# Retention, heads 1 and 2: V and gate as seven half-size products, three quarters of whose weight sums are added by DMA

## The chip, the cores and the metric

The kernel runs on one core of one Trainium2 chip. A core has TensorE (matmul), VectorE, ScalarE, GpSimd (Pool) and SyncE (which here issues the loads), an on-chip memory (SBUF) of 128 partitions, a small accumulator memory (PSUM) that TensorE writes, and 16 DMA engines. The metric is device time of the one core, in microseconds, the median of several runs.

## The reference

A decoder trunk in float32: SEQ = 512 tokens, D_MODEL = 1024, one retention layer with an FFN, then one attention layer with an FFN. The change touches only the retention layer's projections. Each of four heads has 256 columns for q and k and 512 for v and for the gate g:

```python
def retention_mixer(h, w_in, w_out, gn_gain, pos):
    proj = h @ w_in
    q = proj[..., :dqk].reshape(B, S, RET_HEADS, RET_QK_DIM)
    k = proj[..., dqk:2 * dqk].reshape(B, S, RET_HEADS, RET_QK_DIM) * (RET_QK_DIM ** -0.5)
    v = proj[..., 2 * dqk:2 * dqk + dv].reshape(B, S, RET_HEADS, RET_V_DIM)
    g = proj[..., 2 * dqk + dv:]
    ...
    y = retention_chunkwise(q, k, v, log_gamma).astype(jnp.float32)
    mu = jnp.mean(y, axis=-1, keepdims=True)
    var = jnp.mean(jnp.square(y - mu), axis=-1, keepdims=True)
    yn = ((y - mu) * lax.rsqrt(var + GN_EPS)).reshape(B, S, dv) * gn_gain
    return (jax.nn.silu(g) * yn.astype(g.dtype)) @ w_out
```

For one head, v and g together are a 512 x 1024 matrix h times a 1024 x 1024 matrix [Wv Wg].

## The kernel before, in words

**Numbers.** A float32 operand is held as two parts, high and low, both of type float32r. One product is three matmuls: high by high, high by low, low by high (`mm3`). The normalised input stands transposed in `hT_hi` and `hT_lo` (8 depth tiles x 512 tokens).

**Weight units.** Weights come in units of 128 x 1024 (512 KB). `fetch` has SyncE load a unit into one of three `raw` buffers. `parts` has ScalarE cast it into `whi` and VectorE subtract to get `wlo`; there are five buffers of each (`WB`). So a load waits for the subtraction three units back, and a cast waits for the last matmul that reads the unit five back.

**Order.** The program's order on each engine is set by a list scheduler from the order in which the code emits work; each engine then executes its own list strictly in order and waits on semaphores. Generators interleave two streams of TensorE work: `_weave` lets `attend` of one head and the projections of the next alternate.

**Retention.** `project(h)` makes the gate (`proj_rows` with silu), q and k (`rotated`: two products of 128 columns, then a rotation on VectorE) and v (`proj_rows` with `split`). `proj_rows` takes four units of 256 depth rows and, for each, four blocks of 128 tokens; each block gathers in its own accumulator (`pm`, four buffers). `attend(h)` makes scores, decay, the product with v, the group norm (`r_gn` on Pool) and the gated result, transposed into `uh` and `ul`. `project_out(h)` multiplies these by four units of `w_out` and adds into `m`. The loop runs, for h = 1 to 3: `attend(h-1)` woven with the gate part of `project(h)`, the rest of `project(h)`, then `project_out(h-1)` (for the last two heads it comes later, woven with `attend(3)`). x stays in four tiles x0 to x3 from the start until the residual is added at the end of retention.

The loop that the change rewrites is this:

```python
for h in range(1, RET_HEADS):
    nxt, u = [], []
    fill = project(h, nxt)
    _weave(attend(h - 1, u, *cur), fill, 2.5)
    _run(fill)
    if h < last:
        _run(project_out(h - 1, u))
    cur = nxt
```

Of the kernel before, what the change touches and what calls it, by code (L numbers as in the profile page):

```python
# [10 lines left out]
F32 = mybir.dt.float32  # L11
# [64 lines left out]
def _run(gen):  # L76
    for _ in gen:
        pass
# [7 lines left out]
def _weave(gen, fill, per):  # L86

    due = 0.0
    for _ in gen:
        due += per  # L90
        while due >= 1:
            due -= 1
            next(fill, None)
# [3 lines left out]
def trunk(ctx: ExitStack, tc: tile.TileContext, a, out):  # L97
# [100 lines left out]
    def split(src, hi, lo, scale=None):  # L198
        if scale is None:
            nc.scalar.copy(out=hi, in_=src)  # L200
            nc.vector.tensor_sub(out=lo, in0=src, in1=hi.bitcast(F32))  # L201
        else:
            nc.scalar.activation(hi, src, AF.Copy, scale=scale)
            nc.vector.scalar_tensor_tensor(
                out=lo, in0=src, scalar=scale, in1=hi.bitcast(F32), op0=ALU.mult, op1=ALU.subtract
            )
# [212 lines left out]
    def retention(pool, post, then, ahead):  # L419
        w_in, w_out = a["ret_w_in"][0], a["ret_w_out"][0]  # L420
        with pool as tmp:
# [40 lines left out]
            def rotated(n0, name):  # L462
                t = tmp.tile([P, 2, SEQ], F32, name=name, tag=name, bufs=1)
                p = []
                for i in range(2):
                    pm = ps.tile([P, 512], F32, name="pm", tag="mm", bufs=4)
                    w = cols_unit(w_in, n0 + i * P)
                    for k in range(KT):
                        mm3(pm, [t[:, blk(k)] for t in w], (hi[:, k, :], lo[:, k, :]), k == 0, k == KT - 1)
                        yield  # L470
                    p.append(pm)
                u = [tmp.tile([P, SEQ], F32, name="t", tag="t", bufs=3) for _ in range(2)]
                for i in range(2):
                    nc.vector.tensor_mul(out=t[:, i, :], in0=p[i], in1=rot[:, 0, :])
                    nc.vector.tensor_mul(out=u[1 - i], in0=p[i], in1=rot[:, 1, :])
                nc.vector.tensor_sub(out=t[:, 0, :], in0=t[:, 0, :], in1=u[0])
                nc.vector.tensor_add(out=t[:, 1, :], in0=t[:, 1, :], in1=u[1])
                return t

            def project(h, res):  # L480
                g = [tmp.tile([P, 512], F32, name="g", tag="g", bufs=4) for _ in range(NB)]
                v = [[tmp.tile([P, 512], F32R, name=n, tag=n, bufs=4) for n in ("vh", "vl")] for _ in range(NB)]
                yield from proj_rows(
                    4 * D + h * 512, lambda b, p: nc.scalar.activation(g[b], p, AF.Silu), first=h == 0
                )
                if h == 0:
                    nc.sync.dma_start(out=rot, in_=a["rot"])
                    load_cols(0)
                    load_cols(1)
                q = yield from rotated(h * 256, "q")  # L490
                k = yield from rotated(D + h * 256, "k")
                yield from proj_rows(2 * D + h * 512, lambda b, p: split(p, *v[b]))
                res += [q, k, v, g]

            def attend(h, u_, q, k, v, g):
                tag = "po" if h < last else "mm"
# [77 lines left out]
            _run(project(0, cur))  # L574
            for h in range(1, RET_HEADS):
                nxt, u = [], []
                fill = project(h, nxt)
                _weave(attend(h - 1, u, *cur), fill, 2.5)
                _run(fill)
                if h < last:  # L580
                    _run(project_out(h - 1, u))
                cur = nxt
            fill = project_out(last - 1, u)
            u = []
# [559 lines left out]
```

## Time and profile before

| | us |
|---|---|
| median of 3 runs | 1696.15 (1696.0 to 1696.19) |
| the profiled execution, its own time | 1696.22 |
| its span, first to last instruction | 1694.4 |
| TensorE busy, by the page | 1675.3 |
| VectorE busy | 1088.6 |
| head 1's attend to head 2's begin (181.57 to 282.17) | 100.60 |

The page gives busy time by engine, the span in 40 slices, the chain of work that ended last, and the costliest groups of instructions. Matmuls are pipelined, so their recorded durations overlap and their pitch is read from the starts. In a group's row the output stands left of the arrow. Retention takes the span up to about 434 us; its four attends begin at 80.98, 181.57, 282.17 and 360.80 us.

### The profile page before, as it was taken

Reading aid. Unit: us, or ns where it says so; the run is one execution under the profiler, and the core shown is the slowest. Engines: PE = TensorE matmul, PEld = TensorE weight load, DVE = VectorE, ACT = ScalarE, POOL = GpSimd, SP = SyncE. Lnnn points to the kernel's source line nnn. Section 1 sums busy time; section 2 is a strip of 40 time slices with the busy share of each in tenths; the row PEclk is TensorE's granted clock in tenths of the full one; section 3 lists DMA queues with packets and bytes.
Section 4 is the critical chain, followed back from the end, with each engine's and each line's share of the span. In section 5 each row is a group of like instructions: output and inputs, shape, how many; then the busy total and the mean of one; then the engine's idle time right before and its main releaser. Section 6 shows DMA issues by size and latency. Waiting matters only on the chain.

```text
span 1694.4 us, 21845 instructions
## 1 busy us (share of the span) xinstructions
PE 1675.3 (99%) x8494; PEld 1388.9 (82%) x8494; DVE 1088.6 (64%) x1758; ACT 662.8 (39%) x1170; POOL 335.8 (20%) x241
## 2 busy tenths in 40 slices
PE   8999999999999999999999999999999999999998
PEld 6888888887888888888888888888887888888886
DVE  4554545557675777968856466556565865777785
ACT  5332322325445343334254244244254545443441
POOL 1000000001100000024456666565530300000000
PEclk9999999999999999999999999999999999999999
DMA  6422223214514323332322222222221633243141
GB/s 208 126 81 88 81 95 91 82 63 137 175 62 125 112 72 114 99 119 80 111 75 75 76 75 78 77 71 81 80 75 49 196 105 112 63 124 114 36 149 50
DMA packets 208567, 164.52 MB, mean 97 GB/s; under 512 B 5246, under 2 KB 182350, under 8 KB 208463
## 3 DMA queue, kind: packets, MB, share of 16 engines
q1 hardware_dynamic: 208462, 163.12, 31.0%
q8 instruction: 67, 1.10, 0.3%
q14 instruction: 38, 0.30, 0.1%
HBM read 156.81 MB, written 6.29 MB: 96 GB/s over the span
## 4 chain that ended last, share of the span: by engine, by line
PE 93%; DVE 3%; issue 2%; POOL 1%; ACT 1%; DMA 0%; SPq 0%; POOLq 0%; DVEq 0%; ACTq 0%
PE pm L210 22%; PE pm L212 22%; PE pm L211 22%; PE po L210 6%; PE po L211 6%; PE po L212 6%; PE sc L881 2%; PE po L991 2%; PE pt L971 2%; PE s L504 1%; DVE wlo L171 1%; POOL r_rms L217 1%; DVE x L354 1%; ACT junk L223 1%; PE y L210 1%
## 5 line engine op out<-in xcount | busy, mean ns | idle before, releaser
L210 PE MATMUL pm<-hT_hi,whi 128*128 128x512 f32 (+1 forms) x1424 | 544.6, 382 | 0.0
L211 PE MATMUL pm<-hT_lo,whi 128*128 128x512 f32 (+1 forms) x1424 | 537.9, 378 | 1.8 <-DVE hT_lo L201 1.8
L212 PE MATMUL pm<-hT_hi,wlo 128*128 128x512 f32 (+1 forms) x1424 | 538.1, 378 | 1.5 <-DVE wlo L171 1.5
L171 DVE TENSOR_TENSOR wlo<-raw,whi 128x1024 fp32r<-128x1024 f32 x299 | 398.5, 1335 | 212.9 <-ACT whi L170 211.2
L170 ACT CAST whi<-raw 128x1024 fp32r<-128x1024 f32 x299 | 313.1, 1051 | 496.7 <-PE pm L211 254.5
L212 PEld LDWEIGHTS pm<-hT_hi,wlo 128*128 128x128 f32 x1424 | 267.9, 188 | 52.0 <-DVE wlo L171 1.9
L210 PEld LDWEIGHTS pm<-hT_hi,whi 128*128 128x128 f32 x1424 | 268.1, 188 | 50.5 <-issue 2.7
L211 PEld LDWEIGHTS pm<-hT_lo,whi 128*128 128x128 f32 x1424 | 268.2, 188 | 50.2 <-DVE hT_lo L201 3.0
L160 POOL TENSOR_TENSOR raw<-raw,cols 128x1024 f32<-128x1024 f32 x72 | 144.3, 2007 | 465.7 <-DVE al L201 302.1
L210 PE MATMUL pm<-whi,hT_hi 128*128 128x512 f32 (+1 forms) x384 | 141.9, 369 | 0.0
L211 PE MATMUL pm<-wlo,hT_hi 128*128 128x512 f32 (+1 forms) x384 | 136.6, 356 | 0.0
L212 PE MATMUL pm<-whi,hT_lo 128*128 128x512 f32 (+1 forms) x384 | 136.6, 356 | 0.0
L227 POOL TENSOR_SCALAR v_rms<-ss 128x1 f32<-128x1 f32 x31 | 19.9, 643 | 466.1 <-ACT junk L223 450.4
L273 DVE TENSOR_TENSOR m<-po,m 128x512 f32<-128x512 f32 x112 | 75.2, 687 | 40.4 <-PE po L212 39.7
L210 PE MATMUL po<-whi,ah 128*128 128x512 f32 x224 | 87.3, 390 | 0.0
L212 PE MATMUL po<-whi,al 128*128 128x512 f32 x224 | 87.2, 389 | 0.0
L211 PE MATMUL po<-wlo,ah 128*128 128x512 f32 x224 | 87.1, 389 | 0.0
L210 PEld LDWEIGHTS pm<-whi,hT_hi 128*128 128x128 f32 x384 | 72.9, 190 | 11.6 <-issue 1.0
L211 PEld LDWEIGHTS pm<-wlo,hT_hi 128*128 128x128 f32 x384 | 72.9, 190 | 10.9 <-DVE wlo L171 0.7
L212 PEld LDWEIGHTS pm<-whi,hT_lo 128*128 128x128 f32 x384 | 72.8, 190 | 10.7 <-DVE hT_lo L201 0.3
L217 POOL TENSOR_TENSOR r_gn<-v_gn,nhalf 128x1 f32<-128x1 f32 x16 | 8.8, 548 | 357.4 <-DVE v_gn L534 357.4
L612 DVE SCALAR_TENSOR_TENSOR conv<-pm,cols,conv 128x511 f32<-128x511 f32 x88 | 65.7, 746 | 7.9 <-ACT conv L609 6.7
(163 smaller groups left out, 2182.5 us busy)
## 6 DMA issues: line engine op xcount, KB each, us to landing
raw<-in_ffn_w_up SPq DMA_DIRECT2D x88, 512.0 KB, 3.8
raw<-in_att_w_kv SPq DMA_DIRECT2D x48, 512.0 KB, 3.9
raw<-in_ret_w_in SPq DMA_DIRECT2D x47, 512.0 KB, 3.8
raw<-in_ffn_w_down SPq DMA_DIRECT2D x44, 512.0 KB, 3.4
raw<-in_att_w_q SPq DMA_DIRECT2D x24, 512.0 KB, 3.8
raw<-in_ret_w_out SPq DMA_DIRECT2D x16, 512.0 KB, 3.3
away<-x SPq DMA_DIRECT2D x8, 512.0 KB, 3.8
x<-away SPq DMA_DIRECT2D x8, 512.0 KB, 4.6
```

Source lines behind the costliest of these rows:

```text
L160: nc.gpsimd.tensor_mul(out=dst, in0=dst, in1=gain.unsqueeze(2).broadcast_to(list(src.shape)))
L170: nc.scalar.copy(out=hi, in_=raw)
L171: nc.vector.tensor_sub(out=lo, in0=raw, in1=hi.bitcast(F32))
L210: nc.tensor.matmul(o, lhsT=l[0], rhs=r[0], start=start, stop=False)
L211: nc.tensor.matmul(o, lhsT=l[0], rhs=r[1], start=False, stop=False)
L212: nc.tensor.matmul(o, lhsT=l[1], rhs=r[0], start=False, stop=stop)
L217: behind.append(nc.gpsimd.tensor_tensor(out=r, in0=v, in1=nhalf, op=ALU.pow).ins)
L273: nc.vector.tensor_add(out=dst, in0=src, in1=dst)
L612: nc.vector.scalar_tensor_tensor(out=t[:, d:], in0=pg[:, : SEQ - d], scalar=cw(i, f), in1=t[:, d:], op0=ALU.mult, op1=ALU.add)
L881: nc.tensor.matmul(pm[h][:, i, c], lhsT=q, rhs=k, start=True, stop=True)
L971: nc.tensor.transpose(out=pt[:, h, n, :], in_=p[:, h, :], identity=ident)
L991: nc.tensor.matmul(dst, lhsT=v, rhs=p, start=i == 0 and g == 0, stop=i == 7)
```

## The change

Heads 1 and 2 compute v and gate as a 2 x 2 block product. The rows are halved (tokens 0 to 255 and 256 to 511), the depth is halved, and the columns are halved into v and gate. Seven products of half size, numbered 1 to 7, replace eight. Products 1, 2 and 4 take blocks of h as they are. Products 3, 5, 6 and 7 take sums and differences of blocks of h (`block_sums`). These are made once, while head 0 projects, and kept split in the tiles of x, of the gains and of `h`; x is loaded again while head 3 projects, and the two gains too are loaded later.

On the weights' side the signs are chosen so that only plain sums occur: W11 + W12 (product 5), that plus W22 (6), that plus W21 (4), and W12 + W22 (7). The first is added by VectorE into the tile `t1`. W12 is copied into `t3` by ScalarE. The other three sums come from DMAs issued by Pool that add onto `t1` and `t3` as they land (`onto`), in halves of 512 KB, six in each head. Each sum is split again by `parts`. `evac` puts the products together: v and gate gather in float32 tiles, the gate's with its sign turned, which the silu undoes by scale -1.

The turn of a head changes as well: `attend(h-1)` is now woven with q and k of head h (`keys_queries`), then comes product 1, then `project_out(h-1)`, then products 3, 2, 5, 7, 6 and 4. Head 3 still uses `project`, and head 0 too.

```diff
@@ -488,9 +488,138 @@
                     load_cols(0)
                     load_cols(1)
                 q = yield from rotated(h * 256, "q")
+                if h == 0:
+                    block_sums(0)
                 k = yield from rotated(D + h * 256, "k")
+                if h == 0:
+                    block_sums(1)
                 yield from proj_rows(2 * D + h * 512, lambda b, p: split(p, *v[b]))
                 res += [q, k, v, g]
+            sums = []
+            def block_sums(c):
+                if c == 0:
+                    for i in range(4):
+                        sh = const.tile([P, 4, 256], F32R, name=f"s{i}", tag=f"x{i}")
+                        if i < 2:
+                            sl = norm.tile([P, 4, 256], F32R, name="sl", tag="gain", bufs=2)
+                            sums.append((sh, [sl[:, 0:2, :], sl[:, 2:4, :]]))
+                        else:
+                            sl = [norm.tile([P, 2, 256], F32R, name="sl", tag="h", bufs=HB) for _ in range(2)]
+                            sums.append((sh, sl))
+                e, o = slice(c * 2, c * 2 + 2), slice(4 + c * 2, 6 + c * 2)
+                t0, t1 = slice(0, SEQ // 2), slice(SEQ // 2, SEQ)
+                n = [tmp.tile([P, 512], F32, name="t", tag="t", bufs=3).rearrange("p (k n) -> p k n", k=2) for _ in range(3)]
+                whole = lambda dst, k, ts: nc.vector.tensor_add(
+                    out=dst, in0=hi[:, k, ts].bitcast(F32), in1=lo[:, k, ts].bitcast(F32)
+                )
+                put = lambda i, src: split(src, sums[i][0][:, e, :], sums[i][1][c])
+                whole(n[0], e, t1)
+                whole(n[1], o, t1)
+                nc.vector.tensor_sub(out=n[1], in0=n[1], in1=n[0])
+                put(0, n[1])
+                whole(n[2], e, t0)
+                nc.vector.tensor_sub(out=n[0], in0=n[2], in1=n[0])
+                put(2, n[0])
+                nc.vector.tensor_add(out=n[1], in0=n[1], in1=n[2])
+                put(1, n[1])
+                whole(n[2], o, t0)
+                nc.vector.tensor_sub(out=n[2], in0=n[1], in1=n[2])
+                put(3, n[2])
+            def v_gate(h, res):
+                cols_ = 2 * D + h * 512, 4 * D + h * 512
+                g = [tmp.tile([P, 512], F32, name="g", tag="g", bufs=4) for _ in range(NB)]
+                v = [[tmp.tile([P, 512], F32R, name=n, tag=n, bufs=4) for n in ("vh", "vl")] for _ in range(NB)]
+                res += [v, g]
+                load = lambda j, c, u: fetch(cols_of(w_in, cols_[c], 4, (j * 4 + u * 2) * P))
+                kept = {}
+                def onto(t, j, c, u):
+                    nc.gpsimd.dma_start(
+                        out=t[:, u, :].rearrange("p (k n) -> p k n", k=2),
+                        in_=cols_of(w_in, cols_[c], 4, (j * 4 + u * 2) * P),
+                        accum_op=ALU.add,
+                    )
+                def left(i, k, r):
+                    if i in (1, 2, 4):
+                        ts = slice((i == 4) * 256 + r * P, (i == 4) * 256 + (r + 1) * P)
+                        return [t[:, k + 4 * (i != 1), ts] for t in (hi, lo)]
+                    sh, sl = sums[{5: 0, 6: 1, 7: 2, 3: 3}[i]]
+                    return sh[:, k, blk(r)], sl[k // 2][:, k % 2, blk(r)]
+                def evac(i, r, pm):
+                    if i in (1, 3, 5):
+                        if i == 1:
+                            kept[i, r] = tmp.tile([P, 512], F32, name="t", tag="t", bufs=3)
+                        else:
+                            kept[i, r] = g[r + (2 if i == 5 else 0)]
+                        nc.scalar.copy(out=kept[i, r], in_=pm)
+                    elif i in (2, 4):
+                        t = tmp.tile([P, 512], F32, name=f"c{r}", tag=f"s{'hl'[r]}0", bufs=1)
+                        nc.vector.tensor_add(out=t, in0=pm, in1=kept[1, r])
+                        split(t, *v[r + (2 if i == 4 else 0)])
+                    elif i == 7:
+                        kept[7, r] = tmp.tile([P, 512], F32, name=f"c{r}", tag=f"s{'hl'[r]}0", bufs=1)
+                        nc.scalar.copy(out=kept[7, r], in_=pm)
+                    else:
+                        s1, s3, s5, s7 = (kept[j, r] for j in (1, 3, 5, 7))
+                        nc.vector.tensor_sub(out=s1, in0=s1, in1=pm)
+                        nc.vector.tensor_add(out=s5, in0=s5, in1=s1)
+                        nc.vector.tensor_add(out=s3, in0=s3, in1=s5)
+                        nc.scalar.activation(s3, s3, AF.Silu, scale=-1.0)
+                        nc.vector.tensor_add(out=s5, in0=s5, in1=s7)
+                        nc.vector.tensor_add(out=s1, in0=s1, in1=s7)
+                        nc.scalar.activation(s5, s5, AF.Silu, scale=-1.0)
+                def product(i, w):
+                    for r in range(2):
+                        pm = ps.tile([P, 512], F32, name="pm", tag="mm", bufs=4)
+                        for k in range(4):
+                            mm3(pm, left(i, k, r), [t[:, half(k % 2)] for t in w[k // 2]], k == 0, k == 3)
+                        evac(i, r, pm)
+                product(1, [parts(load(0, 0, u)) for u in range(2)])
+                yield
+                w3 = [parts(load(1, 1, u)) for u in range(2)]
+                w2 = [parts(load(1, 0, u)) for u in range(2)]
+                t1, t3 = (
+                    tmp.tile([P, 2, D], F32, name=n, tag=tag, bufs=1) for n, tag in (("t1", "uh"), ("t3", "ul"))
+                )
+                for u in range(2):
+                    r11, r12 = load(0, 0, u), load(0, 1, u)
+                    nc.scalar.copy(out=t3[:, u, :], in_=r12)
+                    nc.vector.tensor_add(out=t1[:, u, :], in0=r11, in1=r12)
+                    onto(t3, 1, 1, u)
+                product(3, w3)
+                w5 = [parts(t1[:, u, :]) for u in range(2)]
+                product(2, w2)
+                for u in range(2):
+                    onto(t1, 1, 1, u)
+                w7 = [parts(t3[:, u, :]) for u in range(2)]
+                product(5, w5)
+                w6 = [parts(t1[:, u, :]) for u in range(2)]
+                for u in range(2):
+                    onto(t1, 1, 0, u)
+                product(7, w7)
+                product(6, w6)
+                w4 = [parts(t1[:, u, :]) for u in range(2)]
+                product(4, w4)
+                yield
+            def keys_queries(h, res):
+                q = yield from rotated(h * 256, "q")
+                k = yield from rotated(D + h * 256, "k")
+                res += [q, k]
 
             def attend(h, u_, q, k, v, g):
                 tag = "po" if h < last else "mm"
@@ -574,11 +703,21 @@
             _run(project(0, cur))
             for h in range(1, RET_HEADS):
                 nxt, u = [], []
-                fill = project(h, nxt)
-                _weave(attend(h - 1, u, *cur), fill, 2.5)
-                _run(fill)
                 if h < last:
+                    fill = keys_queries(h, nxt)
+                    _weave(attend(h - 1, u, *cur), fill, 2.5)
+                    _run(fill)
+                    vg = v_gate(h, nxt)
+                    next(vg)
                     _run(project_out(h - 1, u))
+                    _run(vg)
+                else:
+                    fill = project(h, nxt)
+                    _weave(attend(h - 1, u, *cur), fill, 2.5)
+                    _run(fill)
+                    for b in range(NB):
+                        x[b] = const.tile([P, D], F32, name=f"x{b}", tag=f"x{b}")
+                        nc.sync.dma_start(out=x[b], in_=a["x"][blk(b), :])
                 cur = nxt
             fill = project_out(last - 1, u)
             u = []
```

Two engines show how the listed order moves. First Pool, from the last two group norms of head 0's attend to head 1's; `r_gn` is the group norm's reciprocal root, and the brackets say which engine or DMA semaphore a row waits for. Before:

```order
L217 TENSOR_TENSOR r_gn_841<-v_gn_839,nhalf_76 128x1 [waits DVE_49]
L217 TENSOR_TENSOR r_gn_893<-v_gn_891,nhalf_76 128x1 [waits DVE_49]
L217 TENSOR_TENSOR r_gn_1482<-v_gn_1480,nhalf_76 128x1 [waits DVE_49]
L217 TENSOR_TENSOR r_gn_1506<-v_gn_1504,nhalf_76 128x1 [waits DVE_49,Pool_49]
L217 TENSOR_TENSOR r_gn_1561<-v_gn_1559,nhalf_76 128x1 [waits DVE_49,Pool_49]
```

The same place now:

```order
L217 TENSOR_TENSOR r_gn_886<-v_gn_884,nhalf_76 128x1 [waits DVE_49]
L217 TENSOR_TENSOR r_gn_938<-v_gn_936,nhalf_76 128x1 [waits DVE_49]
L547 DMA t3_1229<-in_ret_w_in 128x2x512 [waits DVE_49,PE_49,Activation_49]
L547 DMA t1_1228<-in_ret_w_in 128x2x512 [waits DVE_49]
L547 DMA t3_1229<-in_ret_w_in 128x2x512 [waits Activation_49]
L547 DMA t1_1228<-in_ret_w_in 128x2x512 [waits DVE_49]
L547 DMA t1_1228<-in_ret_w_in 128x2x512 [waits DMASW1_49,DVE_49]
L547 DMA t1_1228<-in_ret_w_in 128x2x512 [waits DMASW3_49,DVE_49]
L217 TENSOR_TENSOR r_gn_1569<-v_gn_1567,nhalf_76 128x1 [waits DVE_49]
```

Six DMAs stand between the two heads' norms: W22's halves onto `t3` and `t1` in turn, then W21's halves onto `t1`, which wait for W22's landing and for VectorE's split of it.

Second ScalarE, from the end of head 1's projections: before, the last units of v and `w_out` are cast and v leaves its accumulators.

```order
L170 CAST whi_1203<-raw_1200 128x1024 [waits DMAHW3_49,PE_49,Activation_49]
L170 CAST whi_1241<-raw_1238 128x1024 [waits DMAHW4_49,PE_49,Activation_49]
L170 CAST whi_1247<-raw_1244 128x1024 [waits DMAHW5_49,DVE_49,PE_49]
L170 CAST whi_1253<-raw_1250 128x1024 [waits DMAHW6_49,DVE_49,PE_49]
L170 CAST whi_1259<-raw_1256 128x1024 [waits DMAHW7_49,DVE_49,PE_49]
L200 CAST vh_669<-pm_1106 128x512 [waits PE_49]
L200 CAST vh_671<-pm_1107 128x512 [waits PE_49]
```

Now, from the second unit of product 5 (`whi_1277`) through both units of product 7 (`whi_1317`, `whi_1321`) and of product 6 (`whi_1353`, `whi_1357`) to those of product 4:

```order
L600 COPY t3_1229<-raw_1239 128x1024 [waits DMAHW7_49]
L170 CAST whi_1277<-t1_1228 128x1024 [waits DVE_49,Activation_49]
L170 CAST whi_1317<-t3_1229 128x1024 [waits DMASW0_49,Activation_49]
L200 CAST vh_1020<-c1_1310 128x512 [waits DVE_49]
L170 CAST whi_1321<-t3_1229 128x1024 [waits DMASW2_49,PE_49,Activation_49]
L566 COPY g_1016<-pm_1324 128x512 [waits PE_49]
L170 CAST whi_1353<-t1_1228 128x1024 [waits DMASW1_49]
L566 COPY g_1017<-pm_1338 128x512 [waits PE_49]
L170 CAST whi_1357<-t1_1228 128x1024 [waits DMASW3_49]
L573 COPY c0_1375<-pm_1362 128x512 [waits PE_49]
L573 COPY c1_1390<-pm_1377 128x512 [waits DVE_49,PE_49]
L170 CAST whi_1433<-t1_1228 128x1024 [waits DMASW4_49]
```

The casts of products 7, 6 and 4 wait for landings of Pool's DMAs (DMASW) instead of SyncE's loads (DMAHW), and the copies that empty the accumulators stand between them in ScalarE's list.

## Prediction

> **What bounds the kernel now.** I read the page from the top: the span, the busy times, the slices and the shares of the chain that ended last. Then I took a window for each stage of retention, and the timeline of TensorE inside one window.
>
> ```profile
> span 1694.4 us, 21845 instructions
> PE 1675.3 (99%) x8494; PEld 1388.9 (82%) x8494; DVE 1088.6 (64%) x1758; ACT 662.8 (39%) x1170; POOL 335.8 (20%) x241
> PE   8999999999999999999999999999999999999998
> PE 93%; DVE 3%; issue 2%; POOL 1%; ACT 1%; DMA 0%; SPq 0%; POOLq 0%; DVEq 0%; ACTq 0%
> ```
>
> TensorE is 93% of the chain, and the page has no slice in which another engine sets the pace for long. A busy TensorE alone proves little, since its records overlap, so the windows come next. Their columns are the length, then busy time and count for each engine, the granted clock, the share of the DMA engines and GB/s.
>
> ```profile
> 27.00:80.98 53.98, 53.98 (x243) 44.73 (x242) 24.21 (x30) 18.11 (x21) 0.00 (x0) 1.00 0.46 138
> 181.57:282.17 100.60, 100.60 (x447) 82.04 (x447) 51.27 (x84) 28.62 (x46) 2.19 (x4) 1.00 0.28 87
> 282.17:360.80 78.63, 78.63 (x351) 64.01 (x351) 44.30 (x75) 24.59 (x40) 2.19 (x4) 1.00 0.33 104
> ```
>
> The second row is one head's turn (attend of head 1, projections of head 2, output of head 1). TensorE has no gap in it, the clock is full, VectorE is half idle (51.27 of 100.60) and so is the rest. So a matmul taken out of this stage is worth its whole pitch, as long as nothing new makes TensorE wait. The pitch is read where V of head 2 begins and where the output projection follows it, 96 matmuls later:
>
> ```profile
> 238.28 0.39 PE L210 MATMUL pm<-whi,hT_hi 128*128 128x512 f32 x1
> ...
> 260.04 0.39 PE L210 MATMUL po<-whi,uh 128*128 128x512 f32 x1
> ```
>
> (260.04 - 238.28) / 96 = 0.2267 us; the 0.39 is latency and overlaps.
>
> **What the change removes.** V and gate of one head are 2 x 4 blocks x 8 depth tiles x 3 = 192 such matmuls before. Seven products of 2 row blocks x 4 tiles x 3 are 168. Two heads save 48 x 0.2267 = **10.9 us**. All of it lies on the path. Each product takes 24 x 0.2267 = 5.44 us.
>
> **What it adds, and where it lies.** Durations of the added VectorE and ScalarE work, and how closely one follows another:
>
> ```profile
> 59.86 0.68 DVE L475 TENSOR_TENSOR t<-pm,rot 128x512 f32<-128x512 f32 x1
> 60.46 0.68 DVE L477 TENSOR_TENSOR k<-k,t 128x512 f32<-128x512 f32 x1
> ...
> 76.66 1.23 DVE L171 TENSOR_TENSOR wlo<-raw,whi 128x1024 fp32r<-128x1024 f32 x1 [4.21 <-ACT whi L170]
> 77.81 0.68 DVE L201 TENSOR_TENSOR vl<-pm,vh 128x512 fp32r<-128x512 f32 x1
> ```
>
> ```profile
> 98.94 1.05 ACT L170 CAST whi<-raw 128x1024 fp32r<-128x1024 f32 x1 [0.37 <-PE pm L212]
> 99.90 0.36 ACT L203 ACTIVATE uh<-pt,cols 128x128 fp32r<-128x128 f32 x1
> ```
>
> Back to back, a 128x512 VectorE operation costs 0.60, a 128x1024 one 1.15, a 128x1024 cast 0.96 us; the brackets give idle time before a row and what ended it. Whoever waits for the result waits the full 0.68, 1.23 or 1.05.
>
> *Block sums, once, beside head 0's projections.* 24 VectorE operations, 24 x 0.60 = 14.4 us, and 8 casts. The first window has 54 us with 24.2 busy, so VectorE goes to about 39. The tightest point is the accumulator of the third V block, which needs the rotation of K to have left it: that rotation now comes after 7.8 us of VectorE work, sums for the most part, and ends 2.9 us ahead of need. Cost nothing; without that slack, what is late comes one to one.
>
> *Per head:* 14 weight units instead of 8 (6 x 1.15 on VectorE, 6 x 0.96 on ScalarE), 2 sums and 2 copies of 128x1024, 14 more 128x512 operations for putting the products together. That is 6.9 + 2.3 + 8.4 = 17.6 us more on VectorE in a turn with 49 idle. The sum fits; its place is the question, since the chains below pass through it.
>
> *x again, four loads, before head 3's attend:* they wait for the last product that reads each sum and have over 30 us until the residual needs x. Nothing, but the first stands in SyncE's queue ahead of one weight load of head 2.
>
> **The chains that TensorE can now wait for.** The unknown is X, the time from Pool's release to the landing of one 512 KB transfer that adds onto a tile; the kernel before has none, and no DMA at all from Pool. The nearest rows are plain loads of the same matrix, 2 KB a row: landing time in two stretches (around 246 to 282 us and 146 to 182 us), and the work of four of them in a window of 35 us from 145 us on.
>
> ```profile
> L157 SPq DMA_DIRECT2D raw<-in_ret_w_in x4: 368/374/379, 246.3 to 263.1; - x4
> DMA to landing us min/median/max: 3.6/3.6/3.6
> ```
>
> ```profile
> DMA to landing us min/median/max: 4.3/4.3/4.3
> ```
>
> ```profile
> q1 hardware_dynamic: 1088, 2.10, 20.1%
> raw<-in_ret_w_in SPq DMA_DIRECT2D x4, 512.0 KB
> ```
>
> 20.1% of 16 engines over 35 us, by four transfers, is 1.76 us of all 16 for one. An add must also read the tile, so I estimate X = 3.6 + 1.8 = **5.4 us**. The ends are 3.6 (the add costs nothing) and 8.6 (two slow landings, 4.3 + 4.3, one after the other). I take 5.4 as nearest to the row that moves the same bytes.
>
> The ledger of head 1, zero at the end of the output projection of head 0; products follow in the order 3, 2, 5, 7, 6, 4:
> - The three raw buffers hold three units whose split buffers come free only as that projection ends (-2.0, -1.4, -0.7). Their subtractions end at 0.5, 1.6 and 2.75. Each lets a load go. W12's upper half lands at 1.75 + 3.6 = 5.35, the sum with W11 ends at 6.6, and only this frees the buffer for W12's lower half: 6.75 + 3.6 = 10.35, sum at 11.6, cast at 12.7. Product 5 starts at 10.88 and has six matmuls for its first unit (12.24): it waits **0.5**. The low part follows at 13.96, behind five matmuls of the other row block.
> - The copy of W12's lower half ends at 11.43. The add lands at 11.5 + X = 16.9, cast and subtraction end at 19.3. Product 7 starts at 16.8 and wants the low part seven matmuls later, at 18.4: it waits **0.9**, and one more for each us of X above 4.5.
> - ScalarE casts product 6's lower unit only behind that (17.95 + a copy 0.5 + 1.05), its subtraction ends near 20.7, and Pool issues the last add: 20.7 + X = 26.1, split at 28.4. Product 4 starts at 28.6: no wait, but above X = 5.4 again one per us.
> - After that VectorE has 13 operations in a row, and the first transposition of the next attend comes about **0.6** late.
>
> Head 1 waits 2.0. In head 2 an addition of 0.6 lies between the subtractions (the output projection now adds), and the load of x comes ahead of the last raw load (0.5): product 5 waits 1.1, product 7 1.35, product 4 0.15, together 2.6. Behind a waiting cast on ScalarE stand the copies that empty the products' accumulators; there are four, so TensorE does not need them within the wait. Behind Pool's waiting add stand only the next attend's four r_gn, 20 us later.
>
> Sum, against the profiled execution's own 1696.22 (span 1694.4 and 1.8 around it; the median 1696.15 is 0.07 below): 1696.2 - 10.9 + 2.0 + 2.6 = **1689.9 us**. All waits at X are about 4.6 + 4 (X - 5.4): the gain is gone at X = 7.0.
>
> A rule that bears on X: the Trainium skill, "DMA: Bandwidth & Descriptors", section "Anatomy of one DMA", gives for a DMA issued from GpSimd about 2.0 us plus bytes over 436 GB/s. By it, counting the bytes twice, X would be an estimated 4.4 and the sum 1687.3; no run here shows it.
>
> **Rivals.**
> *The adds hide wholly* (X no more than 4.3, the slow plain landing). Left are product 5's waits and 0.4 elsewhere, 2.0 in all: 1687.3. For it: DMA engines are 28% busy in the turn. Against it: the tile must be read too.
>
> *Pool cannot issue while VectorE works.* If each issue waits for one VectorE operation to end, X grows by up to 1.2 (L171's 1.23) to 6.6: waits of 4.4 + 5.0, **1694.7**. VectorE is dense in that stretch. Against it stands what it executes there:
>
> ```profile
> L540 DVE TENSOR_SCALAR u<-u,r_gn x16: 474/486/489, 95.0 to 387.7; 128x512 f32<-128x512 f32 x16
> ```
>
> Only this one-input operation runs faster than the 0.68 of the two-input ones, and it belongs to attend, not to the products. The Trainium skill, "SBUF — State Buffer", section "SBUF: two separate sides", says that a DMA issued from GpSimd cannot get its descriptors written while VectorE runs in a two-port mode. It speaks against this change; by the row above such operations are absent where the adds are issued, and no run here shows the case.
>
> *The add is slow, and this turns the sign.* One mechanism, the two adds in a row onto the same tile (W22, then W21) and the late one onto W12: beyond 5.4 each us of X costs two in each head. From X = 7.0 the change loses, from 7.8 by over 0.2%; at 8.6 the waits are 8.4 + 9.0 and the time **1702.7**. For it: no row shows an add, and the 5.4 holds nothing for Pool's own preparing. Against it: 4.3 + 4.3 lets nothing overlap.
>
> *VectorE becomes the bound.* If its operations did not overlap at their ends (0.68 and 1.23 each), it would run behind through the whole attend of head 1: waits of 7.3 + 4.3, 1697.0. The rows above, 0.60 apart, speak against it.
>
> *The change does not do what it says* can be left aside: the listed order has 48 matmuls fewer on TensorE.
>
> **Chances.** Forecast 0.33, adds hidden 0.18, Pool held up 0.20, slow add 0.24, VectorE bound 0.05. The measurement tells about 0.2%, 3.4 us, from no change. Faster: forecast and hidden adds, 0.52 with a little of the third; same: the rest of the third and the last, 0.23; slower: the slow add, 0.25. The range goes from just under the hidden case, 1686.5, to the slow add at 1703.
>
> **What would show it.** In the profile after: no gap on TensorE ahead of products 3 and 2, one of 0.5 to 1 us at the seventh matmul of product 5 released by ScalarE, one at product 7's second unit released by a DMA through cast and subtraction, little at product 4. The landing of the twelve adds is X itself, and the windows of the two heads must come out 5.4 us minus those gaps shorter. I am wrong if gaps of over 3 us stand at products 7 and 4 (X), if they stand in attend with VectorE busy throughout (VectorE), or if TensorE's pitch in the products is not 0.227.

## The result, and the profile after

| | before | after |
|---|---|---|
| median, us | 1696.08 (1695.85 to 1696.19) | 1708.92 (1707.46 to 1710.21) |
| ratio, 95% interval | | 1.0076 [1.0064, 1.0088] |
| the profiled execution | 1696.22, span 1694.4 | 1708.02, span 1706.2 |

The change costs 12.8 us where 6.3 were to be gained. The profile after, from its page:

```profile
PE 1674.9 (98%) x8446; PEld 1384.4 (81%) x8446; DVE 1136.7 (67%) x1826; ACT 692.5 (41%) x1210; POOL 355.1 (21%) x253
PE   8998998999999999999999999999999999999998
PEclk9999998999999999999999999999999999999999
PE 87%; DVE 5%; DMA 4%; issue 2%; ACT 1%; POOL 1%; POOLq 0%; SPq 0%; DVEq 0%; ACTq 0%
```

The 48 matmuls are gone (8446 for 8494), yet TensorE has two more slices of 8, the granted clock has one, and DMA now carries 4% of the chain that ended last, where it had 0%. The stages, in the order of the three windows shown before (head 0's projections, the turn from head 1's attend to head 2's, the next turn):

```profile
27.00:80.50 53.50, 53.50 (x241) 44.30 (x239) 38.33 (x54) 22.68 (x29) 0.00 (x0) 1.00 0.46 138
185.22:294.36 109.14, 101.17 (x423) 80.09 (x423) 68.46 (x108) 41.30 (x61) 9.44 (x10) 0.95 0.53 142
294.36:372.98 78.62, 78.62 (x351) 63.98 (x351) 48.48 (x82) 27.03 (x44) 2.21 (x4) 1.00 0.35 113
```

The block sums cost nothing: VectorE's 38.33 us lie inside a stage that is not longer than before. The turn of head 2 is 109.14 us where it was 100.60, with 8 us of gaps on TensorE and a clock of 0.95. The turn after it is as before. So all of the loss lies in the two turns with the seven products. Where TensorE waited, in order of time (the brackets give the idle time and what ended it):

```profile
157.81 0.73 PE L210 MATMUL pm<-whi,s 128*128 128x512 f32 x2 [2.42 <-ACT whi L170]
166.83 0.49 PE L210 MATMUL pm<-whi,s 128*128 128x512 f32 x1 [1.68 <-ACT whi L170]
168.09 0.50 PE L211 MATMUL pm<-wlo,s 128*128 128x512 f32 x1 [0.76 <-DVE wlo L171]
...
264.14 0.50 PE L210 MATMUL pm<-whi,s 128*128 128x512 f32 x1 [2.37 <-ACT whi L170]
...
275.17 0.80 PE L210 MATMUL pm<-whi,s 128*128 128x512 f32 x1 [4.13 <-ACT whi L170]
276.43 0.80 PE L211 MATMUL pm<-wlo,s 128*128 128x512 f32 x1 [0.46 <-DVE wlo L171]
```

These are the second units of products 5 (157.81 and 264.14) and 7 (the others), released by a cast, or in the L211 rows by the subtraction that follows it. None stands ahead of products 3 and 2, and product 4 waits 0.17 at most. Behind the casts stand DMAs, as the chain that ended last shows in six of its pieces:

```profile
144.64 5.05 DMA raw<-in_ret_w_in
...
151.07 4.24 DMA raw<-in_ret_w_in
...
156.68 8.96 DMA t<-in_ret_w_in
...
171.40 7.26 DMA t<-in_ret_w_in
...
265.64 13.19 DMA t<-in_ret_w_in
...
281.46 6.32 DMA t<-in_ret_w_in
```

The first two are W12's halves on their way to product 5, the others adding transfers: 156.68 brings product 7 its second unit, 265.64 product 6, and 171.40 and 281.46 are the last adds of the two heads, for product 4. Product 7 of head 2 waits for the add issued just before 265.64, at 263.00, whose cast starts at 274.07. All twelve adds:

```profile
L547 POOL DMA_DIRECT2D t<-in_ret_w_in x12: 1194/1203/1375, 151.1 to 281.5; - x12
DMA to landing us min/median/max: 6.0/8.7/13.2
```

That is X: 6.0 us at best, 8.7 in the middle, 13.2 at worst, of which GpSimd's own instruction takes 1.2. The DMA engines in the stretch from 156 to 169 us, by queue (packets, MB, share of all 16), and the same stretch and head 2's in windows (the last two columns are the DMA share and GB/s):

```profile
q0 software_dynamic: 1088, 2.10, 87.8%
q1 hardware_dynamic: 1584, 0.79, 24.4%
```

```profile
156.00:169.00 13.00, 8.74 (x29) 6.56 (x30) 6.83 (x8) 6.16 (x9) 2.39 (x2) 0.87 1.12 222
262.00:277.00 15.00, 8.27 (x24) 5.98 (x25) 6.82 (x8) 6.24 (x8) 2.41 (x2) 0.81 1.10 256
```

Four adds (2.10 MB) take 0.878 x 13 / 4 = 2.85 us each of all 16 engines. For 13 and 15 us the engines have no free time (a share of 1.1, since records overlap), and yet move 222 and 256 GB/s, less than the 298 that the prediction's plain rows give for full engines (2.10 MB in 20.1% of 35 us). GpSimd issues four adds within 8.2 us, the first and the fourth here:

```profile
151.09 1.38 POOL L547 DMA_DIRECT2D t<-in_ret_w_in  x1 [41.39 <-DVE t L601]
...
159.32 1.19 POOL L547 DMA_DIRECT2D t<-in_ret_w_in  x1 [1.45 <-DVE wlo L171]
```

They ask for 11.4 us of engine time while plain loads ask for more, so each queues behind the last. The second thing that the rows show is the clock: windows at 158 us, and the timeline of TensorE at 169 us.

```profile
158.00:159.00 1.00, 1.00 (x5) 0.77 (x5) 1.00 (x1) 0.00 (x0) 0.00 (x0) 0.87 1.11 201
159.00:161.00 2.00, 2.00 (x6) 1.60 (x5) 0.19 (x2) 1.25 (x2) 1.19 (x1) 0.50 1.11 203
161.00:162.00 1.00, 1.00 (x4) 0.75 (x3) 1.00 (x2) 0.32 (x1) 0.00 (x0) 0.50 1.14 222
162.00:163.00 1.00, 1.00 (x6) 0.83 (x5) 0.66 (x2) 0.00 (x0) 0.00 (x0) 0.93 1.13 216
```

```profile
168.42 0.39 PE L212 MATMUL pm<-whi,sl 128*128 128x512 f32 x1
168.66 0.40 PE L210 MATMUL pm<-whi,s 128*128 128x512 f32 x1
...
169.66 0.63 PE L210 MATMUL pm<-whi,s 128*128 128x512 f32 x1
170.09 0.63 PE L211 MATMUL pm<-wlo,s 128*128 128x512 f32 x1
```

A granted clock of 0.87, 0.50, 0.50, 0.93 puts the half clock from 158.74 to 162.14, 3.4 us, and the pitch goes from 0.24 to 0.43. The trace has four such stretches in retention, after the waits of products 5 and 7 in both heads: three of 3.4 us and a last one of 6.8 (274.8 to 281.6), together 17.1 us. The kernel before has none there.

The sum of the profiled execution: -10.9 for the matmuls; 12.7 of bracketed waits (the six shown, 0.17 at product 4 of head 1 and 0.74 at the next attend's first transposition), with 0.16 more for each of eight, since a bracket counts from the modelled end 0.39 after a start and the pitch is 0.227; and half of the 17.1 us, less the little in which TensorE stood anyway, some 8.0. That is +11.1 of the measured 11.8.

### The profile page after: what moved, and what is told of

Its sections match the earlier page's. It is cut to its first block, busy times and chain, and to the rows that moved or that the text cites. A ratio compares the mean times of both kernels' runs of the same rounds, so it can differ in the third digit from the quotient of the medians.

```text
span 1706.2 us, 21921 instructions
## 1 busy us (share of the span) xinstructions
PE 1674.9 (98%) x8446; PEld 1384.4 (81%) x8446; DVE 1136.7 (67%) x1826; ACT 692.5 (41%) x1210; POOL 355.1 (21%) x253
## 4 chain that ended last, share of the span: by engine, by line
PE 87%; DVE 5%; DMA 4%; issue 2%; ACT 1%; POOL 1%; POOLq 0%; SPq 0%; DVEq 0%; ACTq 0%
PE pm L210 20%; PE pm L212 20%; PE pm L211 20%; PE po L210 6%; PE po L211 6%; PE po L212 6%; DMA t<-in_ret_w_in 2%; PE sc L1020 2%; PE po L1130 2%; DVE wlo L171 2%; PE pt L1110 2%; DMA raw<-in_ret_w_in 1%; PE s L633 1%; POOL r_rms L217 1%; ACT whi L170 1%
## 5 line engine op out<-in xcount | busy, mean ns | idle before, releaser
L211 PE MATMUL pm<-hT_lo,whi 128*128 128x512 f32 (+1 forms) x1424 | 538.0, 378 | 1.8 <-DVE hT_lo L201 1.8
L170 ACT CAST whi<-raw 128x1024 fp32r<-128x1024 f32 x295 | 308.4, 1051 | 426.0 <-PE pm L211 222.4
L211 PEld LDWEIGHTS pm<-hT_lo,whi 128*128 128x128 f32 x1424 | 268.2, 188 | 50.4 <-DVE hT_lo L201 3.0
L210 PE MATMUL pm<-whi,hT_hi 128*128 128x512 f32 (+1 forms) x304 | 107.9, 355 | 0.1
L211 PE MATMUL pm<-wlo,hT_hi 128*128 128x512 f32 (+1 forms) x304 | 105.6, 347 | 0.3 <-DVE wlo L171 0.2
L212 PE MATMUL pm<-whi,hT_lo 128*128 128x512 f32 (+1 forms) x304 | 105.3, 346 | 0.0
L211 PE MATMUL po<-wlo,ah 128*128 128x512 f32 x224 | 87.1, 389 | 0.0
L756 DVE TENSOR_TENSOR act<-conv,pm 128x512 f32<-128x512 f32 x44 | 30.2, 687 | 59.4 <-PE pm L212 51.8
L754 ACT ACTIVATE conv<-conv 128x512 f32<-128x512 f32 x44 | 27.8, 632 | 91.4 <-DVE conv L751 91.3
L210 PEld LDWEIGHTS pm<-whi,hT_hi 128*128 128x128 f32 x304 | 57.9, 190 | 8.4 <-issue 0.8
L211 PEld LDWEIGHTS pm<-wlo,hT_hi 128*128 128x128 f32 x304 | 57.9, 190 | 8.4 <-DVE wlo L171 1.4
```

Source lines behind the costliest of these rows:

```text
L170: nc.scalar.copy(out=hi, in_=raw)
L210: nc.tensor.matmul(o, lhsT=l[0], rhs=r[0], start=start, stop=False)
L211: nc.tensor.matmul(o, lhsT=l[0], rhs=r[1], start=False, stop=False)
L212: nc.tensor.matmul(o, lhsT=l[1], rhs=r[0], start=False, stop=stop)
L756: nc.vector.tensor_mul(out=act, in0=t, in1=pv)
```

## The experiments

Theories, as the expectations name them. **D**: adding transfers fill the DMA engines and queue; their chain sets the end. **C**: the half clock after each wait costs much of it. **V**: VectorE's added work. **P**: the path by GpSimd is slow, adding or not. **L**: one add is slow by itself. **O**: only the order of the loads is wrong. All medians in one table, each against the kernel before on the same chip:

| kernel | us | before | ratio, 95% interval |
|---|---|---|---|
| no adds | 1690.97 | 1695.78 | 0.9971 [0.9959, 0.9983] |
| plain transfers by GpSimd | 1696.90 | 1695.78 | 1.0007 [0.9997, 1.0016] |
| VectorE adds | 1689.36 | 1695.78 | 0.9963 [0.9950, 0.9976] |
| warm | 1713.18 | 1695.78 | 1.0102 [1.0085, 1.0119] |
| VectorE adds, early loads | 1689.09 | 1696.04 | 0.9961 [0.9947, 0.9975] |
| adding transfers, early loads | 1713.77 | 1696.04 | 1.0101 [1.0086, 1.0116] |
| x late | 1708.98 | 1696.04 | 1.0074 [1.0059, 1.0089] |
| half of the adds | 1696.35 | 1696.04 | 1.0003 [0.9994, 1.0012] |
| VectorE adds, direct loads | 1686.91 | 1695.51 | 0.9948 [0.9934, 0.9962] |
| the same, x late | 1686.73 | 1695.51 | 0.9948 [0.9935, 0.9960] |
| adding transfers, direct loads | 1705.30 | 1695.79 | 1.0056 [1.0041, 1.0071] |
| one add in a head | 1691.55 | 1695.79 | 0.9975 [0.9964, 0.9986] |

### No adds

```diff
 def onto(t, j, c, u):
-    nc.gpsimd.dma_start(..., accum_op=ALU.add)
+    return
```

> The twelve adding transfers are left out, so W22 and W21 are missing from the sums and the outputs of heads 1 and 2 are not the reference's; all else stays. Theory D (the adding transfers, 177 ns for a 2 KB packet against 84 for a plain one, fill the DMA engines, and their chain sets the end of both turns): only product 5's waits stay, 0.5 to 1.1 us each, 1687 to 1689 us, and the clock stays full. Theory C (each wait of some 2 us on TensorE also costs 1.7 us by half a clock of 3.4 us, whatever makes it): if product 5 still waits 2.4 us by the raw loads' own chain, each head keeps 2.4 + 1.7, 1693 to 1694. Theory V (VectorE's added work sets the end): within 2 us of 1708.

1690.97 us, between what D and C named; V falls. Product 5's waits stay, 1.72 and 2.07 us, where the prediction had 0.5 and 1.1, here head 1's:

```profile
157.11 0.73 PE L210 MATMUL pm<-whi,s 128*128 128x512 f32 x2 [1.72 <-ACT whi L170]
```

They are the raw loads' own chain. The profiled execution (1689.32) has no half clock in retention, so a wait of this size does not always bring one. It is the fastest of six, which go up to 1692.44.

### Plain transfers by GpSimd

```diff
     in_=cols_of(w_in, cols_[c], 4, (j * 4 + u * 2) * P),
-    accum_op=ALU.add,
```

> The same twelve transfers from GpSimd without the addition: they overwrite the tile, so the sums are lost. Theory D: a packet takes 84 ns instead of 177, landings come to 4 to 6 us, and the time to 1688 to 1693. Theory P (the path by GpSimd is slow, its 1.2 us instruction and its queue, whether or not it adds): landings stay at 6 to 13 us and the time at 1705 to 1709.

1696.90 us. The landings, and the queue's share of the stretch from 151 to 170 us:

```profile
DMA to landing us min/median/max: 4.0/6.2/7.1
```

```profile
q0 software_dynamic: 709, 2.61, 40.5%
```

2.61 MB is five transfers: 0.405 x 19 / 5 = 1.54 us of all engines each, against 2.85 with the addition. They also go out in fewer and larger packets (709 for 2.61 MB, where the adds need 1088 for 2.10). GpSimd's instruction takes 0.72 us where the adding one takes 1.2. The steps so far, in medians against before: no transfers -4.8, plain ones +1.1, adding ones +12.8. So the plain transfers cost 5.9 us and the additions 11.7 more. Neither theory has the number: P's is too high, and D's 1688 to 1693 too low. The same bytes cost nothing when SyncE loads them into raw buffers (next run, 1689.36), so what remains of the cost without the addition is not bytes. What fits is that a transfer into the sum's own tile can start only when the last sum has been read out of it, and a load into a raw buffer runs ahead. No run sends these plain transfers into the tile by SyncE, so GpSimd's share in the 5.9 us stays open.

### VectorE adds

```diff
-    nc.gpsimd.dma_start(..., accum_op=ALU.add)
+    r = load(j, c, u)
+    nc.vector.tensor_add(out=t[:, u, :], in0=t[:, u, :], in1=r)
```

> The twelve additions are made by VectorE from plain loads through SyncE and the three raw buffers; everything is computed. Theory D: product 7's and product 4's waits go, product 5's lower unit comes at 13.8 instead of 12.2 in its ledger, 1.5 to 2.5 us a head, and 1.7 more where that halves the clock: 1688 to 1693. Theory V: 12 x 1.15 = 13.8 us more on VectorE make it slower still, over 1710.

1689.36 us, inside D's range; V falls again. With the same products, sums and order, 19 us less than the changed kernel: the edit only has plain loads through SyncE bring the weights and VectorE add them. Product 5 still waits 1.69 and 2.32 us.

### Warm

```diff
-pm = ps.tile(...)
+pms = [ps.tile(...) for _ in range(2)]   # both accumulators ahead of the loop
...
+ if r == 0 and k == 2:
+     for _ in range({1: {5: 10, 7: 8}, 2: {5: 10, 7: 18}}[h].get(i, 0)):
+         nc.tensor.matmul(pms[1], lhsT=left(i, 1, 0)[0], rhs=w[0][0][:, half(1)], start=True, stop=True)
```

> After with 10 matmuls of no use in product 5's wait and 8 (head 1) or 18 (head 2) in product 7's, into an accumulator that the product then overwrites; everything is computed. Theory C: the four half-clock stretches (17 us in all, 8.5 us of lost TensorE time) go, 1700 to 1702. Theory D: the adds run on at their own pace, so that TensorE, at full clock, only waits longer for them at the next product: 1705 to 1709, with hardly any half clock left.

1713.18 us, higher than either named. The clock is full in head 1's products, and head 2's keep one half clock of 3.4 us, behind product 4:

```profile
141.00:184.00 43.00, 40.55 (x173) 31.83 (x172) 21.96 (x23) 20.46 (x27) 7.37 (x6) 1.00 0.76 170
247.00:297.00 50.00, 43.86 (x179) 34.03 (x178) 23.36 (x26) 20.67 (x25) 7.24 (x6) 0.97 0.76 191
```

Yet nothing is won: the added matmuls take 46 x 0.2267 = 10.4 us, and behind them TensorE waits again, two of the rows being the attend after head 1, which waits for VectorE's row of operations that puts the products together, and product 4 of head 2:

```profile
192.22 1.13 PE L639 MATMUL s<-q,k 128*128 128x256 f32 x4 [1.73 <-DVE t L647]
...
290.89 0.50 PE L210 MATMUL pm<-whi,hT_hi 128*128 128x512 f32 x1 [2.81 <-ACT whi L170]
```

So C as the main cause falls. The reading that fits is that the half clock was spent while the transfers would have been waited for anyway, and the changed kernel's chain that ended last bears it out: in the four half-clock stretches it runs through adding transfers and the casts, subtractions and issues around them, and through halved matmuls only from 168.97 to 169.88. Its exact price stays open, since the added matmuls are themselves on the path and partly outlast the waits.

### VectorE adds, early loads; adding transfers, early loads

The same edit of the order in both, with VectorE's sums in the first and the adding transfers in the second.

```diff
 w3 = [parts(load(1, 1, u)) for u in range(2)]
+first(0)   # W11, W12 upper halves: sum into t1, copy into t3
 w2 = [parts(load(1, 0, u)) for u in range(2)]
-for u in range(2): ...sum, copy, onto(t3, 1, 1, u)
+first(1)
 product(3, w3)
 w5 = [parts(t1[:, u, :]) for u in range(2)]
 product(2, w2)
+for u in range(2):
+    onto(t3, 1, 1, u)
```

> The sums on VectorE as before, with W11's and W12's upper half loaded ahead of W21, so that their raw buffers come free at the end of the output projection instead of after a landing; everything is computed. If product 5's remaining wait of 1.7 and 2.3 us is the chain of raw buffers (load, sum, next load), it goes in both heads and no half clock is left: 1685.5 to 1687.5. If it is VectorE's or ScalarE's own load, the wait stays and the time with it: 1688 to 1691.

1689.09 us, the median hardly other than with the first order (1689.36): the number is that of the second case, but the waits are not. In the profiled execution (1688.06) product 5 waits 0.29 us in head 1 and not at all in head 2, but product 2 now waits 0.75 and 1.4. The wait was the chain of raw buffers, and most of it moved.

> The same order of loads with the adding transfers from GpSimd, as in the change; everything is computed. Theory D (engine time: six adds of 2.8 us and eight plain loads of 1.3 us want 28 of the 33 us that the six products take): product 5 no longer waits, products 7 and 4 still do, 1695 to 1703. Theory O (only the order of the loads was wrong): the waits go as with VectorE's sums, 1686 to 1690.

1713.77 us: O falls outright, D's number was over 10 us too low, and product 5 of head 1 still waits (0.35 and 0.76). An add that is issued earlier takes engine time from W21's lower half, so that product 2 waits:

```profile
264.44 0.79 PE L210 MATMUL pm<-whi,hT_hi 128*128 128x512 f32 x1 [3.63 <-ACT whi L170]
```

### x late

```diff
+late = small.tile([P, 1], F32, name="late", tag="r_gn")
+with tc.issue_after(behind[-1]):
+    nc.gpsimd.tensor_copy(out=late, in_=sums[b][0][:, 0, 0:1].bitcast(F32))
 x[b] = const.tile(...)
```

> The change with the four loads of x held back until the attend after head 2 (GpSimd reads one column of each sum there, four small instructions more); everything is computed. Theory D (the 13.2 us landing in head 2 shares the engines with x): the longest landing falls to 9 or 10 us, product 7's wait in head 2 from 4.1 to 1.5 to 2.5 us, and the time to 1703 to 1706. Theory L (an add is slow by itself, whatever runs beside it): landings and time stay, 1707 to 1710.

1708.98 us, no change, and the longest landing only falls to 12.2. Time and median are those that L named; whether an add is slow by itself, one add in a head measures below.

```profile
DMA to landing us min/median/max: 6.1/8.7/12.2
```

x was not what made head 2's slow landing. The engines stay full without it (9 tenths or more from 262.4 to 277 us), from the adds, the weight loads that run ahead for head 3 and the load of a gain.

### Half of the adds; one add in a head

```diff
 def onto(t, j, c, u):
+    if u:              # half of the adds
+        return
+    if c or not u:     # in the other kernel, instead: one add in a head
+        return
```

> The change with the additions of the lower halves left out (six of the twelve transfers), so the outputs of heads 1 and 2 are not the reference's. Theory D: an add that has the engines to itself lands in 5 to 6.5 us, 1692 to 1698 us in all. Theory L: landings stay at 8 to 9 us, and as the upper halves' adds are in the same chains the time stays over 1700.

1696.35 us: the time is D's, but the landings are not, with a median of 8.6. Of the three adds in a head two are still issued 2.7 us apart behind plain loads.

> The change with one adding transfer left in each head, W21's lower half, which is issued when no plain load is due; the other ten additions are left out, so the outputs of heads 1 and 2 are not the reference's. It measures X by itself: 5.4 us if the prediction's estimate holds for a transfer that is alone, 5.9 to 6.2 by the fastest landing of the change, over 8 if a landing is slow by itself. The time: 1690 to 1693, as without any addition.

1691.55 us, as without any addition, and X by itself:

```profile
DMA to landing us min/median/max: 6.4/6.6/6.9
```

The share of the engines, from 163 to 172 us:

```profile
q0 software_dynamic: 272, 0.52, 38.9%
```

So a lone add takes 6.4 us in head 1, where the engines move nothing else, and 6.9 in head 2, beside a load of x: not 5.4, a little more than the 5.9 to 6.2 that the change's fastest landing named, and not 8.7. It takes 0.389 x 9 = 3.5 us of all engines. L falls: about 2 us of the median landing are company.

### VectorE adds, direct loads, and x late with it; adding transfers, direct loads

```diff
-    r11, r12 = load(0, 0, u), load(0, 1, u)
-    nc.scalar.copy(out=t3[:, u, :], in_=r12)
-    nc.vector.tensor_add(out=t1[:, u, :], in0=r11, in1=r12)
+    for t, c in ((t1, 0), (t3, 1)):
+        nc.sync.dma_start(out=t[:, u, :].rearrange("p (k n) -> p k n", k=2),
+                          in_=cols_of(w_in, cols_[c], 4, u * 2 * P))
+    nc.vector.tensor_add(out=t1[:, u, :], in0=t1[:, u, :], in1=t3[:, u, :])
...
 product(2, w2)
+for u in range(2):
+    onto(t3, 1, 1, u)
```

As with the early loads, the additions onto `t3` now stand behind product 2.

> The sums on VectorE, with W11 and W12 loaded by SyncE straight into the two sum tiles, four loads at once when the output projection leaves them, so that they take no raw buffer and no copy; everything is computed. If the waits that the early order left (0.75 us at product 2, 0.3 at product 5, 1.4 in head 2) come from raw buffers handed on too late, they go and no half clock can follow: 1685.3 + 0.5, that is 1685 to 1687. If four loads at once only crowd the DMA engines (1.4 us of all 16 each), product 5 waits 1 to 2 us again: 1687 to 1691.

1686.91 us, in the first range: 8.6 us below the kernel before and 22 below the changed one. Product 2 no longer waits. Product 5 still does, 0.82 and 0.94 us in the profiled execution, more than with the early order, so that not all waits went as the first range had it: together with 0.29 at the next transposition they are 2.05 us, where the early order left 2.44. The clock stays full:

```profile
141.00:180.00 39.00, 38.18 (x165) 30.48 (x164) 33.83 (x39) 22.93 (x30) 0.00 (x0) 1.00 0.59 189
247.00:276.20 29.20, 28.26 (x121) 22.40 (x120) 28.59 (x34) 15.87 (x21) 0.00 (x0) 1.00 0.82 281
```

In head 2's products VectorE is busy 28.59 of 29.20 us, so little more could be put on it here.

> The same with the four loads of x held back until the attend after head 2; everything is computed. If x in SyncE's queue and on the DMA engines delays head 2's loads, it is 0.5 to 1.5 us below the kernel without this; if not, within 0.5 us of it.

1686.73 us, within 0.2 us of it: x costs nothing where it stands.

> W11 and W12 loaded straight into the two tiles as in the kernel with VectorE's sums, and all twelve additions by GpSimd's transfers again; everything is computed. If a lone add lands in 6 us and two in a row in 9, products 5, 7 and 6 find their weights and only product 4 waits, 3 to 5 us a head with a half clock behind it: 1692 to 1699 us. If adds queue on the DMA engines behind each other and behind plain loads wherever they stand, products 7 and 6 wait as well: over 1700.

1705.30 us, over 1700: product 7 waits in both heads however early its two units are loaded.

```profile
164.99 0.63 PE L210 MATMUL pm<-whi,s 128*128 128x512 f32 x1 [2.42 <-ACT whi L170]
...
270.58 0.50 PE L210 MATMUL pm<-whi,s 128*128 128x512 f32 x1 [3.46 <-ACT whi L170]
```

## Why the prediction was wrong

**What TensorE saves** was right. 10.9 us were predicted; with direct loads and VectorE's sums 8.6 come out in the median, and the waits left in its trace are 0.82, 0.94 and 0.29 us.

**The block sums and x** were right: no cost in the first window, and no difference in the two runs with x late.

**The structure of the ledger** held, its durations did not. With zero at 143.0 us, W12's upper half was to be issued at 1.75 and was at 1.64; the first wait came at product 5's seventh matmul, released by ScalarE, the next at product 7's second unit, and little at product 4, as forecast. The late transposition of the next attend (0.6) came at 0.74.

**Plain landings beside other traffic** were the smaller mis-sized term. The ledger took 3.6 for W12's halves, which landed in 5.05 and 4.24, and put product 5's waits at 0.5 and 1.1 where the trace has 2.42 and 2.37. These 3.2 us are mostly not the adds' doing, since 1.72 and 2.07 stay without any add.

**X was the step that failed.** It was one latency of 5.4 us, the same for each add, as if each had the engines to itself. Alone it is 6.4: GpSimd's instruction takes 1.38 of it, where SyncE's takes 0.37 of the plain 3.6, and for that, as the prediction says, it held nothing. Its upper end of 8.6 ("two slow landings, one after the other") is just the median, and 13.2 lies far outside: the landing times were carried over from rows of a turn in which the engines were 28% busy. The engine time itself was not underestimated (1.76 + 1.8 = 3.5 us for one, where the lone add took 3.5 and each of four in the burst 2.85); what was not added up is that four adds and the plain loads around them are wanted within some 13 us. By the prediction's own sum, 4.6 + 4 (X - 5.4), the median landing gives 17.8 us of waits, 1703.1; with the 3.2 above 1706.3, against 1708.0 in the profiled execution. That this comes so near is luck. Half of the growth, 6.6 us, falls at product 4 by that sum, where the trace has 0.17: the last adds land in 7.26 and 6.32, nearer to the lone one, and TensorE, held up before, comes to product 4 later. And the sum has nothing for the half clock.

**The rivals.** The slow add that turns the sign is what happened, for a reason that the rival did not hold, the queue on the engines. Adds hidden wholly is excluded by the landings. VectorE as the bound is excluded by the runs in which it does six more additions a head and the kernel is faster. GpSimd held up by VectorE was not tried by itself; its instruction takes 1194 to 1375 ns in all twelve cases, among VectorE's work, which leaves it little room. The change's first add, issued at 151.09, has no packet on the engines before 156.2; but plain loads keep them 93% busy from 152.5 on, VectorE itself is idle for 1.34 us from 154.06, and the lone add's first packet came about 2 us after its issue. For the rule of the Trainium skill, "SBUF — State Buffer", section "SBUF: two separate sides", the trace thus has no case, as far as its rows show. The estimate of 4.4 us from the Trainium skill, "DMA: Bandwidth & Descriptors", section "Anatomy of one DMA", differs from the lone add's 6.4, and the measurement decides.

**The half clock** was missed altogether: a wait was priced at its length. By its length it is 8.0 of the 11.8 us, but the chain that ended last holds only 0.9 us of halved matmuls, and the warm run, with one half clock left, is no faster. So it is not shown to be a cause of its own here.

## What to carry to other kernels

Before work is moved to DMA, add up the engine time that every transfer in the stretch wants, and compare it with the stretch; a landing time read from a quieter stretch, or an average share over a whole turn, says nothing about a burst. An addition that an engine with free time makes in 1.15 us from a load that ran ahead was cheaper here than a transfer that adds: this one holds all DMA engines 2.85 to 3.5 us and cannot start before its target has been read. Where loads wait for a shared buffer, a better order in the same buffers mostly moved the wait and left the median where it was, and a place of their own to land in took about 2 us off it; waits of 0.8 to 0.9 us stayed.

## What the runs showed of the hardware

- A DMA that adds onto SBUF takes nearly twice the engine time of the plain one from the same queue (2.85 against 1.54 us of all 16 engines for 512 KB in the bursts measured here; 3.5 for an add alone), and GpSimd 1.2 us to issue instead of 0.72.
- Waits of TensorE well under 3.4 us were followed by half a clock for 3.4 us: 2.42 us at 157.81, and 1.68 with 0.76 shortly after it at 166.83. The Trainium skill, "TensorE: Matmul & The Clock Gate", section "HAM oscillation — how this bites in real kernels", names idle gaps above about 3.4 us; here less was enough. In the profiled executions of all the kernels every single wait of 2.3 us or more was followed by one; 2.05 with x late was, 2.07 without adds was not, and 1.88 and less by itself was not. The length of the half clock, 3.4 us, agrees with the window of 3413 ns that the Trainium skill gives on that page, section "What's actually happening", and the four starts in the changed kernel (158.73, 168.97, 264.55 and 274.79) lie whole multiples of 3.413 us apart.
- Kernels with several such waits spread more from run to run: 1707.46 to 1710.21 after, 1709.97 to 1714.94 with the adding transfers and early loads, against 1712.97 to 1713.39 with the warm clock and 1695.85 to 1696.19 before. Of VectorE's sums the runs with a mean clock of 0.999 took 1687.99 to 1689.36 us, those with 0.998 1690.35 and 1691.04; the last is the profiled one and has one half clock, behind the wait of 2.32. That the place of a wait in the clock's own windows makes the difference fits, and is not shown.
